# A two-layer attention trunk: TensorE in program order in the first attention, 24 conditioning columns on TensorE, a third raw buffer, bias vectors on 128 partitions

## The chip, the cores and the metric

The kernel runs on one core of one Trainium2 chip. The metric is the device time of one execution in microseconds (us). The core has five engines with a queue each: TensorE (PE in the profile, with PEld for its weight loads), VectorE (DVE), ScalarE (ACT), GpSimd (POOL) and SyncE (SP), which only issues DMAs here. ACT issues a few DMAs too. Each queue is worked off in order.

## The reference, cut to what matters

A decoder trunk of two layers, 512 tokens by 1024 features, float32. Each layer's input, residual gate and MLP are set by a conditioning vector c. Layer 0 has two sparse attentions in parallel (NSA with 8 heads, DSA with 8 heads), layer 1 a differential attention; a squared-ReLU MLP follows each.

```python
def reference(x, c, rel_bias, ada_w, ada_b, ...):
    c_act = jax.nn.silu(c)
    for l in range(DEPTH):                                   # 2
        ada = c_act @ ada_w[l] + ada_b[l]                    # 1024 x 6144 a layer
        sh1, sc1, g1, sh2, sc2, g2 = jnp.split(ada, 6, axis=-1)
        h = modulate(x, sh1, sc1)
        if l % 2 == 0:
            y = even_mixer(h, ..., rel_bias)                 # NSA and DSA
        else:
            y = diff_mixer(h, ..., rel_bias, lambda_init)
        x = layer_norm(ALPHA * x + (1.0 + g1[:, None, :]) * y, ln_g[l, 0], ln_b[l, 0])
        h = modulate(x, sh2, sc2)
        y = sq_relu_mlp(h, mlp_w1[l], mlp_w2[l])
        x = layer_norm(ALPHA * x + (1.0 + g2[:, None, :]) * y, ln_g[l, 1], ln_b[l, 1])
    return x
```

A bias from a table of 32 buckets by 16 heads, picked by the distance of two tokens, is added to every attention logit.

## The kernel before

**Weights.** All weights go through one stream (`Stream`, from line 107), a list of items of 128 partitions by 1024 floats (512 KB). `issue` (L134) puts the next items' DMAs on SP's queue as long as a raw buffer is free. There are two lasting raw buffers (`raw0`, `raw1` in `run`), four early ones that leave the pool when the items 24 and after "dq3" are reached, and later ones in tiles of other uses. `prepare` makes of a raw item two float32r parts: the first a cast on ACT (L265), the second a subtraction (L266) on DVE or, in the first attention, mostly on POOL. A product is three matmuls, first by first, first by second, second by first (`mm3`, L350 to L352). Items of kind "w" (compression weights, `cw1`) are used from the raw buffer itself, at most four at a time.

**Conditioning.** `ada` has 48 columns of 128 values a layer; each column of layer 0 is an item. Columns 0 to 15 (shift and scale of the first input) are needed first and are multiplied and summed on DVE (L250). Columns 16 to 39 of layer 0 (the gate, then shift and scale of the MLP) have two ways: a product on POOL (L247) with a sum on ACT (L248), which 21 take, or L250 on DVE for the three in `PLAN['ax']`. Their bias is added per eight columns (`ada_bias`, L407). Columns 40 to 47 of layer 0 and all of layer 1 go through `ada_pair` on TensorE: for two columns, eight matmuls with 32 output columns (L422), an ACT copy out of PSUM (L425), two one-column matmuls on that copy (L427), and a DVE addition of the bias (L428). A pair holds two raw buffers until it is done. `gate_row` spreads a gate over the partitions with 8 matmuls (L438).

**Stages.** From 0 to some 60 us, `even` loops over eight weight blocks "b1": modulated input (L1051 to L1053), then the projections in eight PSUM banks. After the eighth block `bias_write` follows its modulation on ACT's queue: a DMA of the bias vectors (L606) and two of the decay vectors (L608). They had been made by `bias_vectors` (L603: one-hot matmuls of the table, in 16 and 8 partitions) and are written to DRAM with 23 and 8 repeats; `gtile` (L537) and `cmp_bias` (L1214) read them back on SP's queue as bias tiles.

Then come slots of a software pipeline written out by hand, some 50 for NSA and, in a second loop, 19 for DSA. In a slot of NSA stand: gating (L1277, POOL), scores (`s0`: L504, L505), softmax pieces on DVE (L514) and ACT (L517), probabilities transposed (`s2`: L1479) two slots later, products with the values (`pv`: L1297, L1305) four slots later, and pieces of the index scores (L1157) and of a top-k of 16 rounds (L1183, L1184), both on DVE. The projections left ("iq", "ks", ... in the order of `PLAN['ord']`, then "dq0" to "dq3") and the block compression (L1527, in eight steps) are fills: a list with due slots (`Fill`), from which each slot takes its share. `latent_t` (L1106) is a fill behind "vc". An "a" in `ord` is the place of one of the columns 16 to 23 among the items; columns 24 to 39 stand behind the output weights ("eo0" to "eo3", four each).

**Order.** What the code says is the program order. A planner then sets the order of every engine's queue from its own costs: an instruction whose inputs it takes as ready may go ahead of one that the code has earlier. `add_manual_dep` with NoSync, or `issue_after`, lets an instruction stand behind another in the queue without a wait.

## Time and profile before

| | us |
|---|---|
| median of 3 runs | 1448.98 (1446.71 to 1451.75) |
| the profiled execution | 1449.99 |
| its span | 1448.2 |
| PE busy | 1342.0 (93%) |
| PEld busy | 1124.3 (78%) |
| DVE busy | 1143.5 (79%) |
| ACT busy | 658.8 (45%) |
| POOL busy | 581.0 (40%) |

The span is what the trace covers, from its first instruction to its last. Busy times of one engine are unions, so they never exceed the span. In the chain of work that ended last PE has 67% of the span, DVE 19%, DMA 4%. The first attention with its projections lies between 60 and 380 us; layer 0's MLP follows until some 770, layer 1's attention until some 1060, its MLP until the end. A line number in a row is that of the kernel before. "SPq" or "ACTq" is a queue's own instruction, mostly the issue of a DMA.

### The profile page before, as it was taken

Reading aid. Unit: us, or ns where it says so; the run is one execution under the profiler, and the core shown is the slowest. Engines: PE = TensorE matmul, PEld = TensorE weight load, DVE = VectorE, ACT = ScalarE, POOL = GpSimd, SP = SyncE. Lnnn points to the kernel's source line nnn. Section 1 sums busy time; section 2 is a strip of 40 time slices with the busy share of each in tenths; the row PEclk is TensorE's granted clock in tenths of the full one; section 3 lists DMA queues with packets and bytes.
Section 4 is the critical chain, followed back from the end, with each engine's and each line's share of the span. In section 5 each row is a group of like instructions: output and inputs, shape, how many; then the busy total and the mean of one; then the engine's idle time right before and its main releaser. Section 6 shows DMA issues by size and latency. Waiting matters only on the chain.

```text
span 1448.2 us, 22535 instructions
## 1 busy us (share of the span) xinstructions
PE 1342.0 (93%) x8286; PEld 1124.3 (78%) x8286; DVE 1143.5 (79%) x2185; ACT 658.8 (45%) x1412; POOL 581.0 (40%) x432
## 2 busy tenths in 40 slices
PE   6979998899899999999999799999979899999985
PEld 4758666676589888888887687887769789999974
DVE  6678979767578778878789825888975997898898
ACT  2455565746355333333332536776565443333321
POOL 2242677716432444444453622124164523122234
PEclk9989999999999999999999899999989999999997
DMA  9852432423731554444542442332350233323311
GB/s 333 247 165 94 152 104 90 131 72 106 258 132 37 183 178 172 175 175 161 189 163 91 149 153 92 102 103 78 137 166 14 90 100 117 110 70 113 116 59 58
DMA packets 58625, 189.47 MB, mean 131 GB/s; under 512 B 7778, under 2 KB 8482, under 8 KB 58516
## 3 DMA queue, kind: packets, MB, share of 16 engines
q1 hardware_dynamic: 55840, 184.67, 37.5%
q10 hardware_dynamic: 2676, 3.38, 1.1%
q8 instruction: 65, 1.06, 0.3%
q14 instruction: 44, 0.36, 0.1%
HBM read 178.42 MB, written 9.60 MB: 130 GB/s over the span
## 4 chain that ended last, share of the span: by engine, by line
PE 67%; DVE 19%; DMA 4%; issue 4%; ACT 3%; POOL 2%; SPq 0%; DVEq 0%; ACTq 0%; POOLq 0%
PE ps_mm L350 9%; PE ps_mm L351 9%; PE ps_mm L352 9%; PE ps_o L350 4%; PE ps_o L351 4%; PE ps_o L352 4%; PE ps_s L350 3%; PE ps_s L351 3%; PE ps_s L352 3%; PE ps_t L352 2%; PE ps_t L350 2%; PE ps_t L351 2%; DVE b L266 2%; PE ps_s L504 2%; PE ps_o L1297 2%
## 5 line engine op out<-in xcount | busy, mean ns | idle before, releaser
L350 PE MATMUL ps_mm<-hT,b 128*128 128x256 f32 (+1 forms) x560 | 190.9, 343 | 19.2 <-ACT b L265 13.1
L351 PE MATMUL ps_mm<-hT,b 128*128 128x256 f32 (+1 forms) x560 | 189.5, 339 | 5.4 <-DVE hT L717 5.1
L352 PE MATMUL ps_mm<-hT,b 128*128 128x256 f32 (+1 forms) x560 | 188.7, 338 | 1.8 <-DVE b L220 1.8
L350 PEld LDWEIGHTS ps_mm<-hT,b 128*128 128x128 f32 x560 | 108.5, 194 | 35.3 <-ACT b L265 13.1
L351 PEld LDWEIGHTS ps_mm<-hT,b 128*128 128x128 f32 x560 | 108.7, 194 | 18.1 <-DVE hT L717 5.6
L220 POOL TENSOR_TENSOR b<-s,b 128x512 fp32r<-128x512 f32 x33 | 46.9, 1423 | 183.6 <-ACT b L219 179.7
L517 ACT ACTIVATE z<-z,st 128x128 f32<-128x128 f32 (+3 forms) x160 | 89.3, 559 | 65.2 <-DVE st L514 56.5
L896 POOL TENSOR_TENSOR ot<-z,ot 128x512 fp32r<-128x512 f32 x39 | 61.3, 1572 | 141.4 <-ACT ot L895 127.8
L352 PEld LDWEIGHTS ps_mm<-hT,b 128*128 128x128 f32 x560 | 108.3, 194 | 12.0 <-DVE b L220 2.0
L350 PE MATMUL ps_o<-b,ot 128*128 128x512 f32 x251 | 101.1, 403 | 4.0 <-ACT b L265 2.3
L351 PE MATMUL ps_o<-b,ot 128*128 128x512 f32 x251 | 99.9, 398 | 2.9 <-DVE b L266 2.9
L731 DVE TENSOR_TENSOR u<-ps_o,u 128x512 f32<-128x512 f32 x121 | 82.3, 680 | 22.9 <-PE ps_o L352 22.6
L352 PE MATMUL ps_o<-b,ot 128*128 128x512 f32 x251 | 99.3, 396 | 0.0
L514 DVE CUSTOM_DVE_ANT_0 z<-ps_s,g 128x128 f32<-128x128 f32 (+3 forms) x160 | 75.2, 484 | 24.6 <-PE ps_s L505 19.0
L265 ACT CAST b<-raw 128x1024 fp32r<-128x1024 f32 (+1 forms) x62 | 64.3, 1042 | 61.6 <-issue 14.4
L266 DVE TENSOR_TENSOR b<-s,b 128x1024 fp32r<-128x1024 f32 x47 | 70.6, 1505 | 18.7 <-ACT b L265 18.3
L265 ACT CAST b<-s 128x1024 fp32r<-128x1024 f32 x47 | 49.0, 1048 | 78.1 <-PE ps_t L351 15.8
L266 DVE TENSOR_TENSOR b<-raw,b 128x1024 fp32r<-128x1024 f32 (+1 forms) x42 | 55.3, 1318 | 33.6 <-ACT b L265 33.3
L350 PE MATMUL ps_s<-b,ot 128*128 128x512 f32 x181 | 72.8, 402 | 0.0
L351 PE MATMUL ps_s<-b,ot 128*128 128x512 f32 x181 | 72.0, 398 | 0.0
L731 DVE TENSOR_TENSOR u<-ps_s,u 128x512 f32<-128x512 f32 x87 | 59.2, 681 | 15.8 <-PE ps_s L352 15.6
L352 PE MATMUL ps_s<-b,ot 128*128 128x512 f32 x181 | 71.6, 396 | 0.0
(471 smaller groups left out, 4241.4 us busy)
## 6 DMA issues: line engine op xcount, KB each, us to landing
s<-mlp_w SPq DMA_DIRECT2D x55, 512.0 KB
s<-ada_p SPq DMA_DIRECT2D x39, 512.0 KB
s<-mlp_wp SPq DMA_DIRECT2D x33, 512.0 KB
raw<-ada_w SPq DMA_DIRECT2D x23, 512.0 KB
raw<-mlp_w SPq DMA_DIRECT2D x21, 512.0 KB
raw<-mlp_wp SPq DMA_DIRECT2D x19, 512.0 KB
early<-ada_w SPq DMA_DIRECT2D x17, 512.0 KB
raw<-ada_p SPq DMA_DIRECT2D x17, 512.0 KB
```

Source lines behind the costliest of these rows:

```text
L220: (nc.gpsimd if PLAN["sl"][it.l][n] else nc.vector).tensor_tensor(out=lo, in0=src, in1=f32(hi), op=ALU.subtract)
L265: nc.scalar.copy(out=hi.cols(c.start, w), in_=raw[:, c])
L266: getattr(nc, ("vector", "gpsimd")[PLAN["lo"][it.name]] if it.name in PLAN["lo"] else k.lo_engine).tensor_sub(out=lo.cols(c.start, w), in0 ...
L350: mm(ps, lhsT=l[0], rhs=r[0], start=start, stop=False)
L351: mm(ps, lhsT=l[0], rhs=r[1], start=False, stop=False)
L352: mm(ps, lhsT=l[1], rhs=r[0], start=False, stop=stop)
L504: mm(ps, lhsT=q[:, qs], rhs=k[0][:, ks], start=start, stop=False)
L514: i = nc.vector.tensor_tensor_reduce(out=z[:, :w], in0=ps, in1=bias, scale=-1.0, scalar=3e38, op0=ALU.add, op1=ALU.min, accum_out=st[:, m: ...
L517: j = nc.scalar.activation(out=z[:, :w], in_=z[:, :w], func=AF.Exp, scale=-1.0, bias=st[:, m:m + 1], accum_out=st[:, 2 + m:3 + m])
L731: self.nc.vector.tensor_add(out=u[:, sl], in0=ps, in1=u[:, sl])
L896: (nc.gpsimd if PLAN["hl"][l][f % 2] else nc.vector).tensor_tensor(out=hl[:, c0:c1], in0=r[:, c0:c1], in1=f32(hh[:, c0:c1]), op=ALU.subtract)
L1297: nc.tensor.matmul(o[ab], lhsT=V[:, br, j, 64 * ab:64 * ab + 64], rhs=pts[ab][br][:, 128 * j:128 * j + 128], start=i % 2 == 0 and br == 0 ...
```

## The change

It has four parts. (1) TensorE's instructions are traced through `InOrder`, which, where `on` is set, puts each behind the one before it: from the first slot of NSA to the end of DSA TensorE issues in program order. Before and after that the planner's order stays. (2) Columns 16 to 39 of layer 0 go through `ada_pair`, so the old branch on POOL and ACT, `PLAN['ax']` and `ada_bias` go; the eight "a" stand in twos in `ord`, and the host's layout of the columns follows. `cact`, now needed for columns 0 to 15 alone, shares the space of the gate rows. (3) A third lasting raw buffer. (4) The table is repeated eight times over its columns, so that the one-hot matmuls give the bias vectors on 128 partitions and the decay vectors on 64; the vectors are written with 3 repeats from each of 128 partitions (24 in all, for 23), the decay vectors once from each of 64; and the writes stand behind the seventh modulation instead of the eighth.

The diff, cut to its core (further lines that only replace `nc.tensor` by `self.pe_` are left out):

```diff
 PLAN = {...
- 'ax': ((0, 19), (0, 36), (0, 38)),
...
- 'ord': ('iq', 'a', 'ks', 'n0', 'a', 'kw', 'a', 'a', 'a', 'a', 'kc', 'vc', 0, 'a', 1, 2, 3, 'n1', 4, 5, 'a', 6, 7,
+ 'ord': ('iq', 'a', 'a', 'ks', 'n0', 'kw', 'a', 'a', 'a', 'a', 'kc', 'vc', 0, 'a', 'a', 1, 2, 3, 'n1', 4, 5, 6, 7,
          'n2', 'n3'),
...
-NREP = 23
+NREP = 24
...
             if not k.ada_pe(l, m):
-                acc = k.adac[:, l, m:m + 1]
-                if bool(16 <= m < 48) != ((l, m) in PLAN["ax"]):
-                    nc.gpsimd.tensor_tensor(out=raw, in0=raw, in1=k.cact, op=ALU.mult)
-                    nc.scalar.activation(out=raw, in_=raw, func=AF.Copy, scale=0.5, accum_out=acc)
-                else:
-                    nc.vector.scalar_tensor_tensor(out=raw, in0=raw, scalar=0.5, in1=k.cact, op0=ALU.mult,
-                                                   op1=ALU.mult, accum_out=acc)
+                nc.vector.scalar_tensor_tensor(out=raw, in0=raw, scalar=0.5, in1=k.cact, op0=ALU.mult,
+                                               op1=ALU.mult, accum_out=k.adac[:, l, m:m + 1])
...
+class InOrder:
+    def __init__(self, tc):
+        self.tc, self.pe, self.on, self.last = tc, tc.nc.tensor, False, None
+
+    def put(self, i):
+        if self.on and self.last is not None:
+            self.tc.add_manual_dep(i.ins, self.last.name,
+                                   mybir.DependencyInfo(mybir.DependencyClass.NoSync, mybir.DependencyReason.DATA), reason="in order")
+        self.last = i.ins
+        return i
+
+    def matmul(self, *a, **kw):
+        return self.put(self.pe.matmul(*a, **kw))
+
+    def transpose(self, *a, **kw):
+        return self.put(self.pe.transpose(*a, **kw))
...
+        self.pe_ = InOrder(tc)
...
-        mm = self.nc.tensor.matmul
+        mm = self.pe_.matmul
...
-    def ada_bias(self, l, sp):
-        sl = slice(8 * sp, 8 * sp + 8)
-        self.nc.vector.tensor_add(out=self.adac[:, l, sl], in0=self.adac[:, l, sl], in1=self.adab[:, l, sl])
...
-        return l > 0 or m >= 40
+        return l > 0 or m >= 16
...
-        return self.a["ada_p"][8 + m if l else m - 40] if self.ada_pe(l, m) else self.a["ada_w"][m]
+        return self.a["ada_p"][32 + m if l else m - 16] if self.ada_pe(l, m) else self.a["ada_w"][m]
...
-        self.cact = C.tile([128, 1024], F32, name="cact")
+        self.cact = self.B.tile([128, 1024], F32, tag="grow", bufs=1, name="cact")
...
-        sb = [self.s4()[:16, :HB] for _ in range(2)]
+        sb = [self.s4()[:, :HB] for _ in range(2)]
 
         def go():
+            rep = self.z()[:33, :192]
+            nc.vector.tensor_copy(out=rep.rearrange("p (m r) -> p m r", r=8), in_=tab[:, :, None].to_broadcast([33, 24, 8]))
             for i, c0, n, m, t0 in ((0, 0, 512, 16, 0), (0, 512, 128, 16, 0), (0, NVEC, HB - NVEC, 8, 16),
                                     (1, 0, 512, 8, 16), (1, 512, HB - 512, 8, 16)):
                 p = self.bank("t")
-                nc.tensor.matmul(p[:m, :n], lhsT=tab[:, t0:t0 + m], rhs=oh[i][:, c0:c0 + n], start=True, stop=True)
-                nc.vector.tensor_copy(out=sb[i][:m, c0:c0 + n], in_=p[:m, :n])
+                self.pe_.matmul(p[:8 * m, :n], lhsT=rep[:, 8 * t0:8 * t0 + 8 * m], rhs=oh[i][:, c0:c0 + n],
+                                 start=True, stop=True)
+                nc.vector.tensor_copy(out=sb[i][:8 * m, c0:c0 + n], in_=p[:8 * m, :n])
         def write():
-            nc.scalar.dma_start(out=self.bvec, in_=sb[0][:, None, :NVEC].to_broadcast([16, NREP, NVEC]))
-            for x, c in ((sb[0][:8, NVEC:], slice(0, HB - NVEC)), (sb[1][:8], slice(HB - NVEC, 16 * NDEC))):
-                nc.scalar.dma_start(out=self.bdec[:, :, c], in_=x[:, None, :].to_broadcast([8, 8, x.shape[1]]))
+            c = NREP // 8
+            nc.scalar.dma_start(out=self.bvec.rearrange("h (r c) n -> (h r) c n", c=c),
+                                in_=sb[0][:, None, :NVEC].to_broadcast([128, c, NVEC]))
+            for x, c in ((sb[0][:64, NVEC:], slice(0, HB - NVEC)), (sb[1][:64], slice(HB - NVEC, 16 * NDEC))):
+                nc.scalar.dma_start(out=self.bdec.rearrange("h r n -> (h r) n")[:, c], in_=x)
...
-            if k == 7:
+            if k == 6:
                 with self.tc.issue_after(act.ins):
                     bias_write()
...
         self.phase = "n"
+        self.pe_.on = True
...
-                self.ada_bias(0, 2)
...
+        self.pe_.on = False
         self.phase = None
         self.lo_engine = "vector"
         for m in (3, 4):
             st.get(I["adaE", 8 * m + 7])
-            self.ada_bias(0, m)
...
-            for s in range(2):
+            for s in range(3):
                 st.raws.append((self.W.tile([128, 1024], F32, name=f"raw{s}"), 1 << 30))
```

## Rows read from the trace of the kernel before

**Rows 1.** Windows: stretch, length; PE, PEld, DVE, ACT, POOL busy; clock; DMA.

```profile
20.00:40.00 20.00, 19.68 (x90) 15.54 (x90) 18.13 (x32) 5.49 (x7) 0.98 (x1) 1.00 0.95 350
60.00:130.00 70.00, 57.62 (x319) 45.62 (x320) 49.58 (x93) 36.60 (x83) 22.78 (x12) 0.85 0.51 152
130.00:190.00 60.00, 55.69 (x420) 43.07 (x420) 57.35 (x168) 30.55 (x75) 32.50 (x31) 0.94 0.41 135
190.00:300.00 110.00, 99.59 (x693) 73.97 (x692) 90.11 (x285) 69.99 (x187) 78.87 (x73) 0.94 0.33 109
300.00:380.00 80.00, 71.15 (x435) 53.01 (x434) 52.49 (x138) 43.84 (x110) 35.99 (x33) 0.97 0.38 120
```

**Rows 2.** The chain that ended last, 0 to 130 us: start, length, what.

```profile
49.48 11.88 DMA bvec<-s
...
66.86 9.87 DMA raw<-ada_w
...
91.85 0.43 PE ps_mm L350
...
99.47 0.23 PE ps_mm L350
```

**Rows 3.** Timeline of ACT, 44 to 100 us: start, length, what [idle, releaser].

```profile
49.48 0.82 ACT L1051 ACTIVATE hT<-z,mod 128x512 fp32r<-128x512 f32 x1 [2.08 <-DVE mod L1049]
...
50.20 5.58 ACTq L608 DMA_DIRECT2D bdec<-s  x2
55.90 1.05 ACT L265 CAST b<-early 128x1024 fp32r<-128x1024 f32 x1 [5.60 <-issue]
...
67.94 1.05 ACT L265 CAST b<-early 128x1024 fp32r<-128x1024 f32 x1 [7.09 <-DMA early<-ev_b]
```

**Rows 4.** The timeline of PE, 44 to 100 us.

```profile
62.30 0.79 PE L350 MATMUL ps_mm<-hT,b 128*128 128x512 f32 x1 [2.77 <-DVE q L373]
...
86.63 0.91 PE L1106 MATMUL ps_t<-ident,ot 128*128 128x128 f32 x3 [6.32 <-DVE ot L1099]
```

**Rows 5.** Lines 247, 248, 250 (ns min/median/max); line 247's window.

```profile
L247 POOL TENSOR_TENSOR raw<-raw,cact x16: 2344/2376/2420, 73.8 to 293.1; 128x1024 f32<-128x1024 f32 x16
...
L248 ACT ACTIVATE raw<-raw x16: 1041/1048/1064, 76.9 to 296.5; 128x1024 f32<-128x1024 f32 x16
...
L250 DVE SCALAR_TENSOR_TENSOR raw<-raw,cact x7: 1205/1220/1807, 15.6 to 286.5; 128x1024 f32<-128x1024 f32 x7
...
190.00:300.00 110.00, 32.83 (x14) 0.94 0.33 109
```

**Rows 6.** The timelines of POOL and DVE, 214 to 228 us, and line 1236 over the span.

```profile
215.23 2.37 POOL L247 TENSOR_TENSOR raw<-raw,cact 128x1024 f32<-128x1024 f32 x1
...
215.18 0.55 DVE L529 COPY s<-ps_t 128x384 f32<-128x384 f32 x1
...
215.91 1.72 DVE L1236 TENSOR_SCALAR cst<-cst 128x4 f32<-128x4 f32 x1
...
L1236 DVE TENSOR_SCALAR cst<-cst x8: 154/226/1715, 152.2 to 245.7; 128x4 f32<-128x4 f32 x8
```

**Rows 7.** Pairs on TensorE: the chain, 376 to 394 us, and line 425 over the span.

```profile
385.82 0.54 PE ps_mm L427 x4
...
389.81 1.86 PE ps_mm L422 x32
...
L425 ACT COPY z<-ps_mm x4: 365/372/372, 384.7 to 391.7; 128x256 f32<-128x256 f32 x4
```

**Rows 8.** The timeline of SP, 125 to 420 us.

```profile
310.85 23.00 SPq L537 DMA_DIRECT2D g<-bvec  x3
```

**Rows 9.** The chain that ended last, 300 to 430 us.

```profile
333.94 5.45 DMA raw<-ev_out
...
366.86 4.43 DMA s<-mlp_w
```

**Rows 10.** The timeline of PE, 150 to 185 us.

```profile
165.52 0.79 PE L504 MATMUL ps_s<-k,q 128*128 128x512 f32 x1 [2.51 <-DVE st L514]
```

More of the change, by code (lines that the diff above doesn't have):

```diff
@@ L437, in row @@
                 c = 4 * h + k
-                nc.tensor.matmul(ps[:, 128 * k:128 * k + 128], lhsT=col[:, c:c + 1].to_broadcast([128, 128]), rhs=self.ident,
+                self.pe_.matmul(ps[:, 128 * k:128 * k + 128], lhsT=col[:, c:c + 1].to_broadcast([128, 128]), rhs=self.ident,
                                  start=True, stop=True)
@@ L502, in scores @@
     def scores(self, ps, q, k, qs, ks, start=True):
-        mm = self.nc.tensor.matmul
+        mm = self.pe_.matmul
         mm(ps, lhsT=q[:, qs], rhs=k[0][:, ks], start=start, stop=False)
@@ L1227, in cmp_a @@
                 for o in range(0, 128, m):
-                    nc.tensor.matmul(ps[o:o + m, 32 * s:32 * s + 32], lhsT=f32(nq[4 * k + s])[:, 128 * i + o:128 * i + o + m],
+                    self.pe_.matmul(ps[o:o + m, 32 * s:32 * s + 32], lhsT=f32(nq[4 * k + s])[:, 128 * i + o:128 * i + o + m],
                                      rhs=kc[:, 32 * (s % 2):32 * (s % 2) + 32], start=True, stop=True)
@@ L1296, in pv @@
                     for ab in range(2):
-                        nc.tensor.matmul(o[ab], lhsT=V[:, br, j, 64 * ab:64 * ab + 64], rhs=pts[ab][br][:, 128 * j:128 * j + 128],
+                        self.pe_.matmul(o[ab], lhsT=V[:, br, j, 64 * ab:64 * ab + 64], rhs=pts[ab][br][:, 128 * j:128 * j + 128],
                                          start=i % 2 == 0 and br == 0 and j == 0, stop=False)
@@ L1304, in pv @@
                 for ab in range(2):
-                    nc.tensor.matmul(po[p][64 * ab:64 * ab + 64], lhsT=box["cmp", 1][rs, 64 * ab:64 * ab + 64],
+                    self.pe_.matmul(po[p][64 * ab:64 * ab + 64], lhsT=box["cmp", 1][rs, 64 * ab:64 * ab + 64],
                                      rhs=pc[p // 2][rs, hs], start=False, stop=True)
@@ L1399, in s0 @@
                 if i:
-                    nc.tensor.matmul(ps[:, :w], lhsT=self.negr, rhs=drop[i][:, :w], start=True, stop=False)
+                    self.pe_.matmul(ps[:, :w], lhsT=self.negr, rhs=drop[i][:, :w], start=True, stop=False)
                 self.scores(ps[:, :w], dq[p][ab], dk[p][ab], slice(128 * i, 128 * i + 128), slice(0, w), not i)
@@ L1427, in pv @@
                     for ab in range(2):
-                        nc.tensor.matmul(po[64 * ab:64 * ab + 64], lhsT=Vd[:, j, p, 64 * ab:64 * ab + 64], rhs=PT[p][ab][:, c:c + 128],
+                        self.pe_.matmul(po[64 * ab:64 * ab + 64], lhsT=Vd[:, j, p, 64 * ab:64 * ab + 64], rhs=PT[p][ab][:, c:c + 128],
                                          start=j == 0, stop=j == i)
@@ L1493, in pv @@
                 o = po[64 * ab:64 * ab + 64]
-                self.nc.tensor.matmul(o if both else o[:, 128:], lhsT=v[j], rhs=y, start=j == 0, stop=j == n - 1)
+                self.pe_.matmul(o if both else o[:, 128:], lhsT=v[j], rhs=y, start=j == 0, stop=j == n - 1)
     def compress_in(self, ps, kv):
@@ L1526, in compress @@
                             m = 64 if 1 else 128
-                            nc.tensor.matmul(pss[k][o:o + m], lhsT=w[:, cs + o:cs + o + m], rhs=xl[:, :, 4 * c + li],
+                            self.pe_.matmul(pss[k][o:o + m], lhsT=w[:, cs + o:cs + o + m], rhs=xl[:, :, 4 * c + li],
                                              start=c == 0 and li == 0, stop=c == 3 and li == 3)
@@ L1552, in compress @@
                 if kv == 0:
-                    nc.tensor.matmul(ps[:, :64], lhsT=w2[:, 128 * k:128 * k + 128],
+                    self.pe_.matmul(ps[:, :64], lhsT=w2[:, 128 * k:128 * k + 128],
                                      rhs=h[:, k, 0].rearrange("p g n -> p (g n)"), start=k == 0, stop=k == 1)
                 else:
-                    nc.tensor.matmul(ps[:, :64], lhsT=h[:, k].rearrange("p d g n -> p (d g n)"),
+                    self.pe_.matmul(ps[:, :64], lhsT=h[:, k].rearrange("p d g n -> p (d g n)"),
                                      rhs=w2[:, 256 + 64 * k:320 + 64 * k], start=k == 0, stop=k == 1)
@@ L1685, in s3 @@
                 v = V[h // 4][j // 2][:, 512 * (j % 2) + c:512 * (j % 2) + c + 128]
-                nc.tensor.matmul(po[h][:, i], lhsT=pt[:, js], rhs=v, start=j == 0, stop=j == i)
+                self.pe_.matmul(po[h][:, i], lhsT=pt[:, js], rhs=v, start=j == 0, stop=j == i)
             if i == 3 or h == 7:
```

18 lines of the change are left out of this document (9 added, 9 removed).

## The prediction

> **What bounds the kernel now.** I read the windows view first, for the stretch that the change touches: from 60 us, when the first projection ends, to 380 us, when the first attention's output is normalised. [rows 1] cuts it in four. TensorE is busy 57.62 of 70, 55.69 of 60, 99.59 of 110 and 71.15 of 80 us, so it stands idle 12.4, 4.3, 10.4 and 8.9 us, 36 us in all. DVE is nearly full once, 57.35 of 60 us in 130 to 190. No engine bounds the whole stretch: the first part waits, the second is DVE's, the rest is mostly TensorE's.
>
> Then I read the chain of waits at the opening [rows 2]. From 49.48 the chain is a DMA, the write of the bias vectors, 11.88 us for 920 KB, that is 77 GB/s. SP's queue goes through a read of those vectors to a conditioning load that takes 9.87 us. ACT shows the same congestion [rows 3]: its two issues of the decay vectors last 5.58 us, the cast behind them waits 5.60 us, and a later cast waits 7.09 us for its weights. TensorE pays with 2.77 us of idling at 62.30 and 6.32 us at 86.63 [rows 4]; the granted clock averages 0.85 in 60 to 130 [rows 1], and the spacing of a 512-column matmul is 0.43 us at 91.85 against 0.23 us at 99.47 [rows 2].
>
> Third, the conditioning columns themselves [rows 5]: a column on the old path is 2.38 us of POOL and 1.05 us of ACT, or 1.22 us of DVE. The plan puts 21 of the 24 on POOL and ACT, 3 on DVE. In [rows 6] a POOL product runs from 215.23 for 2.37 us and a four-element DVE operation beside it takes 1.72 us; the same line has a median of 0.226 us. POOL's product thus holds up DVE.
>
> **The change part by part.** The profiled execution took 1449.99 us (span 1448.2); the median of the runs shown is 1448.98, 1.0 us lower. The sum is made on the first and 1.0 us is taken off at the end.
>
> *Bias vectors on 128 partitions, written one step earlier.* The write goes from 920 to 960 KB, the decay writes stay at 264 KB. The rate is bounded below by the 77 GB/s of [rows 2] and above by the 350 GB/s that the loads reach in 20 to 40 us [rows 1]: 1.22 MB take 3.5 to 16 us. I take some 5 us, near the upper rate, because the sources then lie on all partitions, as those of the loads do. One more small DVE copy (33 partitions by 192) costs at most the 0.55 us of a 384-column copy [rows 6]; it comes before the first projection, where the tables' DMAs end last. On ACT's queue the three issues move from behind the eighth modulation to behind the seventh; the cast of the last weight block and the eighth modulation are queued behind them. The eighth waited 2.08 us for DVE anyway [rows 3]: issues up to that long cost nothing, the old 5.58 us would cost 3.5. What can be won is TensorE's idling in 60 to 130, 12.4 us [rows 1], and the lowered clock: a mean of 0.85 between 1.2 and 2.4 GHz is 21 of the 70 us at 1.2 GHz, and where TensorE runs in them, say in half, each matmul takes 0.43 us for 0.23, so 5 us can come back. From 0 to 17 us. Four of the twelve new pairs fall here too and use about 9 us of that room (next but one), so I take -9 us with these four paid.
>
> *POOL, ACT and DVE set free.* 21 products of 2.38 us leave POOL (50 us), 21 x 1.05 us leave ACT (22 us, of which twelve copies of 0.37 us return), 3 x 1.22 us leave DVE, with three small bias additions; twelve additions of two columns come. Most of it was cover already. What counts is DVE held up in 190 to 300, where 14 products run for 32.8 us [rows 5]: if each held DVE for the 1.5 us of [rows 6] and DVE were the path throughout, 21 us; if DVE is never the path, nothing. DVE is busy 90.11 of 110 there, TensorE 99.59 [rows 1], so about a quarter counts: -5 us.
>
> *Twelve pairs on TensorE.* [rows 7] shows the same routine for later columns: 32 records, two pairs, take 1.86 us, so 0.93 us a pair, and its two one-column matmuls 0.54 us: 1.47 us a pair, 17.6 us for twelve. In program order the one-column matmuls stand directly behind the eight, and wait for an ACT copy of 0.37 us. Nothing else can go between. The wait is 0.4 us at least and 1.8 us where a cast of some 1.05 us is ahead on ACT; transposes, scores and projections are queued behind it. So 1.9 to 3.3 us a pair; I take 2.3. The other eight pairs, 18.6 us, fall into 190 to 300, where TensorE idles 10.4 us. The bounds are 8 x 1.9 - 10.4 = +5 and 8 x 3.3 = +26; I take +13, because idle time that is spread over waits covers only part.
>
> A page weighs against this. TensorE's busy share in 190 to 300 leaves 10.4 us of room, its weight loads 36 us (73.97 of 110, [rows 1]). The Trainium skill, "Perfetto Trace Analysis", section "Identifying the Most-Contended Engine", says that matmul occupancy is a poor measure because matmuls are pipelined, and that weight-load occupancy should be used. By that the eight pairs would fit and cost nothing; it is the third rival below.
>
> *A third raw buffer.* SP's queue stands 23.00 us before the reads of the bias rows at 310.85 [rows 8], and the load of the output weights behind it then takes 5.45 us on the chain; a first MLP weight takes 4.43 us at 366.86 [rows 9]. With one more buffer these loads are issued before that wait, or one item sooner. From 0 to -9.9 us; I take -5. A pair holds two buffers until it is done, which is why the third is not worth more. Later stages hold few DMA waits and get 0.
>
> *Program order.* In the stretch before, the planner lets TensorE run ahead: at 86.63 it stands before the transposes of the latent, which the code queues behind the "vc" projection, while index scores of earlier slots are still to come; at 165.52 it stands 2.51 us before scores [rows 4, 10]. Those scores are behind DVE, which program order does not cure; other work that was ready is what it can put there. Outside the opening the idling is 23.6 us [rows 1]. Order could win about half, 12 us. It could also lose: each projection's first matmul waits for its weight's second part, which POOL makes in some 2.4 us, as long as a product [rows 5], and the stretch has thirteen projections (scores and transposes are queued behind them): at half of it 16 us. I take -6.
>
> Sum: -9 - 5 + 13 - 5 - 6 = -12, so 1438.0 us profiled and 1437 us in the median.
>
> **The rivals.** *Slower: TensorE stands at the head of its own queue.* If ACT's casts are in the way of each pair's copy, the pairs cost their upper bound, +26, and order loses 5 instead of winning 6, while the other gains stay: -9 - 5 - 5 + 26 + 5 = +12, 1461 us. For it: 93% busy share in 130 to 190 and 91% in 190 to 300, and the turn-round has no cover. Against: ACT is busy only 69.99 of 110 us and gets lighter. It decides from the point at which pairs and order together cost more than the 19 us of the rest.
>
> *No change: DVE takes what is won.* DVE has 57.35 of 60 us in 130 to 190 and its index and top-k work is unchanged. What is won before 130 then turns into TensorE waiting for DVE: -3 instead of -9, -3 instead of -5, +13, -5, -2: 0, 1449 us. Against: TensorE feeds DVE, and before 130 DVE idles too, 49.58 of 70.
>
> *Faster than forecast: the pairs fit.* Eight pairs in the 36 us of room that the weight loads leave: the +13 becomes 0, the sum -25, 1424 us. Against it, in the chain TensorE's pieces follow each other closely in 190 to 300; for it, half of those pieces run at a lowered clock (0.94 in the mean).
>
> *The change doesn't do what it says*, if the order is kept but the planner fills the other queues so that it gives the same times: it is the forecast without its -6, and lies within the forecast's case.
>
> **How the numbers follow.** About 0.3%, 4.3 us, is what a measurement of this kernel can tell from no change. Forecast (1437): 0.43. Pairs fit (1424): 0.21. No change (1449): 0.15. Slower (1461): 0.21. The range reaches down to -9 more on the opening (its bound of 17, rounded up) and -5 on loads from the third rival, 1410, and up to the slower rival, 1461: below 1 in 10 is left on either side. Faster 0.64, same 0.15, slower 0.21.
>
> **What the profile after would show.** Right: the bias write under 6 us; no ACT issue over 3 us near 46; TensorE idle in the 70 us after the first projection under 6 us; no POOL product and no DVE stretch beside it; pairs of 1.5 us with under 1 us of idling before their one-column matmuls; no load of output weights on the chain. Wrong: TensorE idle before the one-column matmuls for over 1.8 us; long idling before projections that waits for POOL's second part; a first attention in which DVE is 95% busy from 100 to 200 with TensorE waiting; or a bias write that still takes over 10 us.

## The result: 2.9% slower

The changed kernel takes 1488.52 us in the median of four executions (1486.87 to 1495.55) against 1447.85 us before (four executions): a ratio of 1.029, 95% interval 1.0256 to 1.0324. The forecast was 1437 us and the range ended at 1461, so the sign was wrong and the time lies outside the range. The execution profiled after took 1489.86 us, its span is 1488.1 us, 39.9 us longer than before.

All of the loss arises in the first attention. The first statistics of the norm that follows it start at 369.7 us before and at 409.9 us after, 40.2 us later; at the end of the span the distance is 39.9 us. So the same windows as in [rows 1] are the place to look.

The windows of the kernel after (stretch, length; PE, PEld, DVE, ACT, POOL busy; clock; DMA):

```profile
60.00:130.00 70.00, 58.56 (x385) 45.50 (x385) 47.26 (x99) 33.88 (x74) 9.89 (x6) 0.93 0.45 143
130.00:190.00 60.00, 40.58 (x322) 32.65 (x319) 50.64 (x149) 23.44 (x60) 23.61 (x24) 0.83 0.34 103
190.00:300.00 110.00, 92.75 (x742) 71.98 (x741) 72.34 (x258) 50.49 (x146) 38.44 (x56) 0.88 0.21 70
300.00:380.00 80.00, 70.94 (x465) 54.28 (x464) 41.66 (x112) 35.87 (x90) 18.62 (x20) 0.98 0.27 93
```

From 130 to 300 us every engine is *less* busy than in [rows 1] (part of that is the change's own doing on POOL and ACT, which lost the columns). From 130 to 190 us TensorE fell from 55.69 to 40.58 us of 60, DVE from 57.35 to 50.64; from 190 to 300 TensorE fell from 99.59 to 92.75 although four pairs of columns came to it. In this stretch no engine has become the bound; the engines wait for each other. The granted clock fell with it, from 0.94 to 0.83 and from 0.94 to 0.88.

What TensorE waited for after, 55 to 420 us (engine, line, releaser: us in total, times, longest):

```profile
PE ps_mm L297 <- ACT z L436: 8.0, 12, 1.8
PE ps_o L297 <- issue: 8.0, 1, 8.0
PE ps_s L297 <- DVE ot L484: 6.8, 1, 6.8
PE ps_s L297 <- ACT z L1219: 6.8, 7, 4.3
PE ps_mm L297 <- DMA raw<-ada_p: 6.7, 2, 4.7
PE ps_mm L297 <- DVE raw L256: 4.8, 1, 4.8
PE ps_t L300 <- POOL z L1265: 4.7, 2, 3.2
PE ps_o L297 <- DVE ot L1567: 3.3, 1, 3.3
```

There is no single cause: a few long waits for DVE, ACT, POOL and DMA, in all 65.0 us (365 less the 299.98 busy) against 40.2 us before. In time they stand as follows (the timeline of PE after: start, length, what, idle before it and its releaser):

```profile
68.62 1.19 PE L297 MATMUL ps_s<-q,ot 128*128 128x512 f32 x2 [6.77 <-DVE ot L484]
139.16 1.09 PE L297 MATMUL ps_o<-ot 128*128 128x64 f32 x4 [7.97 <-issue]
151.84 0.39 PE L297 MATMUL ps_s<-k,q 128*128 128x256 f32 x1 [4.30 <-ACT z L1219]
180.93 1.09 PE L297 MATMUL ps_o<-ot 128*128 128x64 f32 x4 [3.28 <-DVE ot L1567]
234.51 1.31 PE L300 MATMUL ps_t<-ident,z 128*128 128x128 f32 x3 [3.19 <-POOL z L1265]
248.59 1.94 PE L297 MATMUL ps_mm<-raw,ccol 128*32 128x256 f32 x16 [4.67 <-DMA raw<-ada_p]
283.82 1.51 PE L297 MATMUL ps_mm<-raw,ccol 128*32 128x256 f32 x12 [4.75 <-DVE raw L256]
```

The longest is worth reading through. At 139.16 the last matmuls of the first compression start after 7.97 us of idling. They multiply what the compression's hidden layer gives after its activation, a run of small DVE and ACT pieces. The same stretch on DVE (timeline of DVE after):

```profile
131.90 0.68 DVE L1201 MAX8 m<-ot 128x8 f32<-128x512 f32 x1
...
132.69 0.68 DVE L1202 MATCH_REPLACE8 ot<-m,ot 128x512 f32<-128x512 f32 x1
133.77 2.11 DVE L1557 TENSOR_TENSOR z<-z 128x124 f32<-128x124 f32 x1 [0.41 <-ACT z L1556]
135.81 0.68 DVE L1201 MAX8 m<-ot 128x8 f32<-128x512 f32 x1
136.41 0.20 DVE L1558 TENSOR_SCALAR z<-z 128x124 f32<-128x124 f32 x1
...
138.85 0.21 DVE L1567 TENSOR_SCALAR ot<-z 128x124 f32<-128x124 f32 x1
```

The activation's pieces (lines 1557 to 1567) alternate with the top-k search (lines 1201, 1202), and one of them takes 2.11 us. The last piece ends at 139.06, and 0.1 us later TensorE goes on, although the profile names no releaser ("issue"). TensorE stands 8 us for 1.1 us of matmuls, and index scores, projections and the next units stand behind them in the queue. The piece of 2.11 us runs beside a subtraction for a weight's second part on POOL (timeline of POOL after):

```profile
133.40 2.34 POOL L260 TENSOR_TENSOR b<-raw,b 128x1024 fp32r<-128x1024 f32 x1 [0.42 <-ACT b L259]
```

### The profile page after: what moved, and what is told of

Same layout as the page of the kernel before. It is cut to its first block, busy times and chain, and to the rows that moved or that the text cites. A ratio compares the mean times of both kernels' runs of the same rounds, so it can differ in the third digit from the quotient of the medians.

```text
span 1488.1 us, 22990 instructions
## 1 busy us (share of the span) xinstructions
PE 1350.9 (91%) x8526; PEld 1133.9 (76%) x8526; DVE 1137.1 (76%) x2189; ACT 642.8 (43%) x1382; POOL 523.4 (35%) x411
## 4 chain that ended last, share of the span: by engine, by line
PE 73%; DVE 15%; DMA 4%; ACT 4%; issue 3%; POOL 2%; ACTq 0%; DVEq 0%; SPq 0%; POOLq 0%
PE ps_mm L297 31%; PE ps_o L297 16%; PE ps_s L297 15%; PE ps_t L297 7%; PE ps_t L300 3%; DVE b L260 2%; DVE u L749 1%; ACT b L259 1%; DMA raw<-ev_out 1%; DVE b L219 1%; DVE m L1201 1%; POOL b L260 1%; DVE ot L1202 1%; DVE z L525 1%; DVE hT L735 1%
## 5 line engine op out<-in xcount | busy, mean ns | idle before, releaser
L297 PE MATMUL ps_mm<-hT,b 128*128 128x256 f32 (+1 forms) x1680 | 333.9, 344 | 23.8 <-ACT b L259 13.4
L297 PEld LDWEIGHTS ps_mm<-hT,b 128*128 128x128 f32 x1680 | 265.5, 196 | 61.2 <-ACT b L259 13.4
L297 PE MATMUL ps_o<-b,ot 128*128 128x512 f32 x753 | 199.5, 395 | 4.5 <-DVE b L260 3.0
L297 PEld LDWEIGHTS ps_o<-b,ot 128*128 128x128 f32 x753 | 133.8, 188 | 33.7 <-DVE b L260 3.8
L297 PE MATMUL ps_s<-b,ot 128*128 128x512 f32 x543 | 145.8, 397 | 0.0
L297 PEld LDWEIGHTS ps_s<-b,ot 128*128 128x128 f32 x543 | 98.3, 191 | 18.4 <-DVE u L749 0.5
L297 PE MATMUL ps_mm<-b,ot 128*128 128x512 f32 x384 | 100.9, 410 | 7.1 <-DVE u L749 6.1
L297 PEld LDWEIGHTS ps_mm<-b,ot 128*128 128x128 f32 x384 | 72.3, 196 | 24.5 <-DVE u L749 7.3
L297 PEld LDWEIGHTS ps_t<-q,b 128*128 128x128 f32 x504 | 66.5, 188 | 4.4 <-DVE b L219 0.4
L297 PE MATMUL ps_t<-q,b 128*128 128x256 f32 x504 | 69.2, 282 | 0.1
```

The costliest lines, as they stand in the source:

```text
L297: return self.put(self.pe.matmul(*a, **kw))
```

## The experiments

Two questions: which part of the change loses, and by what mechanism. All ratios are to the kernel before on the same chip.

### Which part: each part undone or done alone

**Without the order.** The changed kernel, everything but the order kept:

```diff
-        self.pe_.on = True
```

> The changed kernel with the planner's order on TensorE again; columns, third buffer and bias vectors as changed. Theory A (program order lets TensorE stand at the head of its own queue, and costs more than all of the loss): 1430 us, 18 below the kernel before, since the opening's gain of some 10 us and POOL's freed time stay. Theory B (the columns on TensorE cost: loads and turn-round of the pairs): 1475 to 1485 us. Theory C (only both together cost: the pairs' waits have no cover in program order): 1440 to 1450 us.

Measured: 1452.14 us against 1452.1, ratio 1.0007 (0.9983 to 1.003). None of the theories names this time: A is 22 us too low, B 23 too high, C 2 too low. The order costs the whole loss, 36 us by the medians and 41 by the ratios (the two kernels come from two series, each beside the kernel before); the other three parts together are worth nothing that can be measured. The same stretches without the order (windows):

```profile
130.00:190.00 60.00, 56.35 (x454) 44.15 (x452) 54.98 (x174) 31.75 (x82) 31.95 (x32) 1.00 0.37 118
190.00:300.00 110.00, 104.86 (x806) 73.99 (x802) 74.84 (x251) 52.86 (x151) 41.82 (x55) 0.94 0.32 105
```

In 130 to 190 TensorE is busy 56.35 us and gets 454 matmul records done where the changed kernel gets 322. At the compression the same chain of small pieces takes as long: its hidden matmuls end at 128.66, its last ones start at 137.14, 8.5 us later (8.0 with the order). But here TensorE idles only 0.61 us of it, because projections, scores and the spreading of a gate stand in front (timeline of PE without the order):

```profile
134.23 0.91 PE L297 MATMUL ps_mm<-hT,b 128*128 128x512 f32 x3
134.99 1.05 PE L297 MATMUL ps_mm<-ident,adac 128*128 128x128 f32 x8
...
137.14 0.63 PE L297 MATMUL ps_o<-ot 128*128 128x64 f32 x4 [0.61 <-PE ps_t L300]
```

Up to the first statistics of the norm the two kernels have nearly the same number of matmul records. The windows from 55 us to that point, with the order and without:

```profile
55.00:409.90 354.90, 293.48 (x2096) 227.46 (x2095) 237.00 (x674) 165.01 (x421) 111.05 (x120) 0.91 0.33 104
```

```profile
55.00:376.10 321.10, 303.69 (x2085) 225.44 (x2085) 230.89 (x673) 162.73 (x421) 114.24 (x120) 0.95 0.36 118
```

With the order TensorE idles 61.4 us and is busy 293.5; without it 17.4 and 303.7. So the 33.8 us between them are 44 us of more idling less 10 us of busy time: by the profile the loss is idling, not slower matmuls.

**The order alone.** The kernel before with the class InOrder and its calls, switched on and off where the change does it:

```diff
-                nc.tensor.matmul(ps[:, 128 * k:128 * k + 128], ...
+                self.pe_.matmul(ps[:, 128 * k:128 * k + 128], ...
...
+        self.pe_.on = True
...
+        self.pe_.on = False
```

> The kernel before with TensorE in program order from the first slot of NSA to the end of DSA, and nothing else. Theory A: 1490 us or more, that is, 40 to 55 us above the kernel before. Theory B: 1440 to 1455 us. Theory C: 1450 to 1465 us, since no pair is in the ordered stretch.

Measured: 1481.21 us, ratio 1.0209 (1.0164 to 1.0254), +29 us. That is 9 us less than theory A's least and 16 or more above B and C: the order loses with the old columns too. TensorE stands 76.3 us between 55 and 420 us, and in one wait for what the change takes away: at 139.7 for ACT's part of a column (line 248), 7.18 us.

**The order in the first half of the stage only.** Switched off before the second of the stage's two attentions (the one that the top-k search masks):

```diff
         ck = box["ck"]
+        self.pe_.on = False
```

> The changed kernel with the order ended between NSA and DSA. The trace of the changed kernel has the first softmax piece of DSA 34.7 us after the last one of NSA, against 7.1 us before. Theory A with its larger part at that join: 1460 us (28 us back). Theory A with its loss inside NSA (20 us are lost there by the last NSA softmax): 1480 us. Theory B: no change, 1488 us.

Measured: 1483.86 us, ratio 1.023 (1.0191 to 1.0269). Some 5 to 9 us of the loss come from the second attention (the intervals of the two ratios overlap, so this share is not clear of noise); the rest, 32 us against no order, from the first, where compression, projections, index scores, top-k and three branches interleave.

**The bias vectors alone.** The kernel before, with the write from 128 partitions one step earlier and nothing else:

```diff
+            rep = self.z()[:33, :192]
...
-            nc.scalar.dma_start(out=self.bvec, in_=sb[0][:, None, :NVEC].to_broadcast([16, NREP, NVEC]))
+            nc.scalar.dma_start(out=self.bvec.rearrange("h (r c) n -> (h r) c n", c=c),
+                                in_=sb[0][:, None, :NVEC].to_broadcast([128, c, NVEC]))
...
-            if k == 7:
+            if k == 6:
```

> The kernel before with the bias vectors on 128 partitions and their write one step earlier, and nothing else. Theory F (the opening's gain of 10 us at the latent's end stays, and the columns eat it in the kernel without order): 1440 us, 8 to 12 below. Theory G (the gain is gone by the first softmax piece of NSA, as in the kernel without order, where it is 0.1 us at that point): 1447 to 1454 us, the same as before.

Measured: 1442.32 us against 1448.82, ratio 0.9936 (0.9913 to 0.9958). This part wins 6.5 us, less than theory F's 8 to 12 and more than G's nothing, and this kernel is faster than both. The windows of 56 to 62 us, first of the kernel before, then of this one:

```profile
56.00:62.00 6.00, 3.52 (x18) 2.85 (x16) 3.04 (x3) 4.85 (x7) 2.40 (x1) 0.97 0.94 123
```

```profile
56.00:62.00 6.00, 6.00 (x30) 5.33 (x29) 2.39 (x3) 3.42 (x5) 2.41 (x1) 1.00 0.94 282
```

The DMA engines are as busy in both (0.94), but they move 282 GB/s instead of 123, and TensorE no longer stands. The two windows don't hold the same transfers. Before, the write is on its way until 61.36 us [rows 2]; here it is issued at 48.21, and SP, which waits for it (`DMA bvec<-s`), issues the first read of it at 55.80:

```profile
55.80 1.35 SPq L537 DMA_DIRECT2D g<-bvec  x2
```

So the write takes some 7.6 us for 960 KB instead of 11.88 for 920, and ends 5.6 us earlier. The spread over the partitions and the earlier place were changed together; no run separates them. The last transpose of the latent starts 5.2 us earlier (84.26 us, before 89.42), and 6.9 us of lead are left at the end of the span.

**The columns, with and without the third buffer.** The changed kernel without the order and with the old bias vectors; then the same with two buffers:

```diff
-            for s in range(3):
+            for s in range(2):
```

> The kernel before with the columns on TensorE and the third raw buffer; old bias vectors, planner's order. Theory F: 1460 us, 8 to 12 above before, since the columns cost what the bias vectors bring. Theory G: 1450 to 1456 us, about the same as before.

> As cols_raw3, with two raw buffers as before. If the third buffer is worth the 5 us of the prediction: 5 us above cols_raw3. If pairs with two buffers have to wait for each other's loads: 10 to 25 us above it. If the buffer is worth nothing: the same as cols_raw3.

Measured: with three buffers 1454.85 us, ratio 1.0045 (1.0024 to 1.0067), +6 us; with two 1468.24 us, ratio 1.0117 (1.0091 to 1.0143), +19 us. The third buffer is worth 13.4 us by the medians, 10.4 by the ratios, once the columns are on TensorE. With the 6.5 us of the bias vectors, the +6.0 of the columns with three buffers makes the nothing that all three parts gave together. The groups of the pairs' matmuls, 55 to 310 us (busy, mean ns, idle before and releaser), with two buffers:

```profile
L297 PE MATMUL ps_mm<-raw,ccol 128*32 128x256 f32 x144 | 12.2, 411 | 8.5 <-DMA raw<-ada_p 8.5
L297 PE MATMUL ps_mm<-sel,z 128*128 128x1 f32 x42 | 7.2, 273 | 1.1 <-ACT z L436 1.1
L297 PE MATMUL ps_mm<-early,ccol 128*32 128x256 f32 x32 | 2.3, 387 | 4.9 <-issue 4.7 <-DVE adac L439 0.2
```

and with three:

```profile
L297 PE MATMUL ps_mm<-raw,ccol 128*32 128x256 f32 x160 | 11.1, 385 | 0.2 <-DVE adac L439 0.2
L297 PE MATMUL ps_mm<-sel,z 128*128 128x1 f32 x44 | 7.4, 269 | 1.1 <-ACT z L436 1.1
L297 PE MATMUL ps_mm<-early,ccol 128*32 128x256 f32 x16 | 1.3, 385 | 0.0
```

With two buffers TensorE waits 13.2 us before pairs: 8.5 for loads, and 4.7 for which the profile names no releaser. With three it does not wait for a load at all. The work itself is 21.7 and 19.8 us. The third buffer without the columns was not tried.

### By what mechanism: who is late, or that nothing may pass

Four theories of the order's cost: the pairs' turn-round carries it (the slower rival of the prediction); the late pieces named above carry it; DVE makes them late, with top-k rounds that run ahead or with top-k as a whole; or, whoever is late, the order takes away what TensorE could do meanwhile, and the next late instruction takes the place of each one that is mended.

**Pairs outside the order; compression and compressed branch outside the order.** In two kernels, one call each as it was:

```diff
 def ada_pair(...)
-        nc, mm = self.nc, self.pe_.matmul
+        nc, mm = self.nc, self.nc.tensor.matmul
```

> The changed kernel with the matmuls of the pairs left out of the order, so that the planner places them; all else keeps program order. Theory A: 1480 us or more, as twelve turn-rounds of 0.65 to 1.8 us make 8 us of TensorE's idling. Theory B and C: 1450 to 1465 us, as the pairs' waits for loads (17 us in three of them) and copies get cover.

```diff
 compression, last matmuls (kv 0 and 1); cmp_c
-                    self.pe_.matmul(ps[:, :64], ...
+                    nc.tensor.matmul(ps[:, :64], ...
-            self.pe_.transpose(pt[:, :128], cb, self.ident)
+            nc.tensor.transpose(pt[:, :128], cb, self.ident)
```

> The changed kernel with three kinds of TensorE instructions left out of the order: the last matmuls of each block compression and the transposes of the compressed branch's probabilities. In the changed kernel TensorE idles 8.0 and 3.3 us before the first two compressions end and 4.7 us before such transposes, 16 us of 65 in 55 to 420 us. Theory D (a few late instructions at the queue's head cost what TensorE idles there, and no more): 1470 to 1475 us. Theory E (whichever instruction is late next takes the place, as with the pairs left out, which gained nothing): 1483 to 1500 us.

Measured: the first 1498.1 us, ratio 1.0332 (1.0292 to 1.0373), no faster than the changed kernel; the second 1484.59 us, ratio 1.023 (1.0199 to 1.0261). So the pairs are not the carrier: their wait for ACT's copy is 8.0 us in twelve in the list above, 0.7 us each. (For loads and prepared buffers the list has 14.2 us in four waits before pairs, 6.7, 4.8 and 2.7, not 17 in three.) And of the 16.0 us of waits before the instructions freed in the second (8.0, 3.3 and 4.7 in the list above) 4 us came back by the medians, 9 by the ratios. The timeline of PE in the second, where the changed kernel waits 4.67 us for a load:

```profile
241.03 1.94 PE L297 MATMUL ps_mm<-raw,ccol 128*32 128x256 f32 x16 [4.54 <-DVE ot L1202]
```

The compression's waits are gone, but three of 2.0 to 2.5 us stand in their place, the wait before this pair has only another releaser, and the branch's transposes still come after 3.19 us although they are free; TensorE idles 54.8 us, 10 less. So a quarter to a half of what these waits cost did come back: theory E's range holds the time, but theory D is not wholly wrong.

**Top-k behind the softmax.** Each round is kept behind the last softmax maximum placed before it:

```diff
-            ta = 0
+            ta = 1
```

> The changed kernel, with one edit: each round of the top-k search on DVE is kept behind the softmax maximum that the program placed last before it, so that the 48 rounds can no longer run ahead. In the changed kernel the last round ends near 165 us of the trace (194 us before), between the pieces of the compression that TensorE, in order, stands waiting for. Theory F (rounds running ahead delay the late pieces on DVE, and the order makes TensorE stand for each): TensorE's idle time between 55 and 420 us falls from 65 us by 10 or more and the time from about 1488 us to 1470 to 1480. Theory E (the order itself, whoever is late: the next late instruction takes the place of each one mended): within 5 us of the changed kernel, 1483 to 1493.

Measured: 1496.62 us, ratio 1.0331 (1.0299 to 1.0364), nothing won, and 4 us above theory E's range. The rounds do run later: the last match-replace starts at 301.6 us, against 248.2 in the changed kernel and 258.5 before (the expectation's 165 is where two of the three blocks of rows are done). But the edit does not touch the longest wait, 7.69 us here: the rounds of the first block stand between the compression's pieces as they did. So this run speaks against rounds that run ahead in general, not against those at the compression; the next pair of runs does.

**Two of sixteen rounds, in order and free.**

```diff
-            todo = [i for i in only if rounds.get(i, 16) < 16]
+            todo = [i for i in only if rounds.get(i, 2) < 2]
...
-            if r == 15:
+            if r == 1:
...
```

> The changed kernel with 2 of the 16 top-k rounds for each of three blocks of rows (42 of 48 rounds, some 1.4 us of DVE each in two instructions of 0.3 to 0.7 us, are left out, so the sparse attention selects fewer keys to drop and the output differs). Read beside the same reduction without the order: the difference of the two is what the order costs when DVE has some 50 us less to do in the stage. Theory F (DVE's top-k rounds make the late pieces late): the order then costs under 15 us of the 37 that it costs with all rounds. Theory E (any work of another engine on the way is late for an engine that stands in order two slots behind): it still costs 25 us or more.

> The changed kernel without the order on TensorE, with 2 of the 16 top-k rounds for each of three blocks of rows (42 of 48 rounds are left out, so the output differs): the partner of the reduced kernel in order. DVE is some 95 per cent busy from 130 to 190 us in the kernel before; were DVE the bound of the stage without the order, about 30 to 45 us would go (1407 to 1422 us); if TensorE is, under 10 (1442 to 1452).

Measured: in order 1484.82 us (ratio 1.024, 1.0206 to 1.0273), free 1442.66 us (0.996, 0.9937 to 0.9982), beside a kernel before of 1449.35. The order costs 42 us with 42 of 48 rounds taken away, no less than with all of them. DVE's load does not carry it. At the compression, where no round stands between the pieces any more, TensorE still waits 6.28 us (timeline of PE, in order):

```profile
139.53 1.08 PE L297 MATMUL ps_o<-ot 128*128 128x64 f32 x4 [6.28 <-ACT z L1560]
```

The windows of 55 to 420 us, in order and free:

```profile
55.00:420.00 365.00, 309.93 (x2228) 239.81 (x2226) 198.46 (x569) 169.69 (x431) 119.82 (x128) 0.92 0.36 118
```

```profile
55.00:420.00 365.00, 350.55 (x2475) 264.89 (x2475) 228.05 (x621) 193.00 (x492) 139.22 (x140) 0.98 0.41 135
```

Free, TensorE idles 14.5 us; in order 55.1 us, with DVE busy little more than half of the time.

**A deeper pipeline.** Transposes three slots behind the scores, products five:

```diff
-        e2, e3 = (2, 4)
+        e2, e3 = (3, 5)
```

> The changed kernel with the first attention's hand-written pipeline one slot deeper: the transposes of a unit's probabilities stand three slots behind its scores instead of two, the products with V five instead of four. Theory D (the depth written by hand is too shallow for an engine that may not look ahead): the transposes' and products' waits shrink, and the time falls by 10 us or more, to under 1478. Theory E: the waits at the compression, at the compressed branch, at the pairs and at the scores stand in other steps of the slot and stay; the time is within 6 us of the changed kernel's, or worse, since the deeper pipeline holds its buffers longer.

Measured: 1496.03 us, ratio 1.0328 (1.0301 to 1.0355), no faster than the changed kernel. The long waits stand where they stood, in other steps of the slot (7.76 us at 136.7 before the compression's last matmul).

**The order by degrees.** Each instruction is kept behind the one K places before it in the program (K = 8, 32, 128, 512; the changed kernel is K = 1):

```diff
-            self.tc.add_manual_dep(i.ins, self.last.name,
+            self.tc.add_manual_dep(i.ins, self.last[-K].name,
...
-        self.last = i.ins
+        self.last.append(i.ins)
```

> The changed kernel with a looser order: each TensorE instruction stands behind the one 8 places before it in the program, not behind the last one. Between 55 and 420 us the changed kernel has 2136 matmuls in 365 us, so 8 places are some 1.4 us of work. The order costs 36 us in all (1488 against 1452). Theory E-near (what is lost is ready work just behind a late instruction; TensorE's longest waits are 2 to 8 us): a quarter to a half of it comes back, 1470 to 1480. Theory E-far (what is lost is work brought forward from far behind): nothing comes back, 1484 to 1492.

> As before with 32 places, some 5.5 us of work at the same rate. Theory E-near: most of the 36 us is back, 1455 to 1466. Theory E-far: at most a quarter, 1478 to 1490.

> As before with 128 places, some 22 us of work, longer than any single wait of TensorE in the changed kernel (8.0 us). Theory E-near: all of it is back, 1448 to 1456, the time without the order. Theory E-far: about half, 1465 to 1475.

> As before with 512 places, some 88 us of work, a quarter of the stage. Both theories: the time without the order, 1448 to 1456. If it is still slower by 10 us or more, the scheduler had brought work forward over more than that, or the manual dependency has a price of its own, whatever it orders.

Measured:

| places that an instruction may be taken early | us | ratio to before (95%) | TensorE idle, 55 to 420 us |
|---|---|---|---|
| 1 (the change) | 1488.52 | 1.029 (1.0256 to 1.0324) | 65.0 |
| 8 | 1502.12 | 1.036 (1.0324 to 1.0396) | 46.1 |
| 32 | 1469.17 | 1.013 (1.0094 to 1.0166) | 31.1 |
| 128 | 1458.61 | 1.0059 (1.0026 to 1.0092) | 24.2 |
| 512 | 1453.67 | 1.0039 (1.0017 to 1.0062) | 23.6 |
| any | 1452.14 | 1.0007 (0.9983 to 1.003) | 22.0 |

The windows of 55 to 420 us behind the last column, for 8 and for 32 places:

```profile
55.00:420.00 365.00, 318.88 (x2104) 232.79 (x2102) 235.44 (x681) 167.52 (x424) 111.97 (x120) 0.89 0.32 102
```

```profile
55.00:420.00 365.00, 333.95 (x2262) 243.71 (x2261) 243.59 (x708) 172.30 (x442) 126.65 (x132) 0.94 0.37 124
```

From 32 places on, the freedom that is given back brings the time back with it: a little over half of the order's loss with 32 places (1.6 of 2.8%), four fifths with 128, nine tenths with 512. With 512 places there are as many added dependencies as with one, so they have no price of their own above the 0.3% that is left. The "near" theory has the larger part, but its forecast for 32 places (1455 to 1466) was missed by 3 us and that for 128 by 3 us: some of what is lost may be work brought forward over more than 128 places. Eight places are slower than one by 14 us (0.7% by the ratios), which no theory expected. TensorE idles 19 us less there in the window, but its work takes longer: up to the first statistics of the norm (416.5 us) it is busy 316.30 us for 2082 records, where the changed kernel is 293.48 for 2096. The granted clock is 0.89 against 0.91. As an estimate from these two means, some 4% more of 360 us is then spent at 1.2 instead of 2.4 GHz, 14 us in which half the work is done: some 7 of the 23 us. Where the rest comes from stays open.

One thing holds for all these runs. The planner sets the queues of the other engines too, and sets them anew for each kernel; no run holds them fixed. How much of the loss is TensorE's own queue, and how much is other engines and loads that the planner then placed later, is not separated.

## Why the prediction was wrong

**The step that failed is the program order: -6 us was taken, with a bound of +16, and it costs +36 or more.** It went wrong twice.

First, the idle time was read the wrong way. The prediction took the 23.6 us of idling outside the opening as what an order could win. But that idling was what was left after the planner had put ready work, most of it from up to some hundred places further on (the order by degrees), in front of instructions that come late. Without the order and with the rest of the change the idling from 55 to 420 us is 22.0 us, with it 65.0 us: 43 us more, and 36 to 41 us of time. For the same work it is 44 us. The wait of [rows 10], 2.51 us before scores, was read correctly as one that order does not cure; but nowhere did the prediction ask the reverse: what work stands in front of a late instruction that order forbids.

Second, the bound was set by one named wait, that of each projection for its weight's second part from POOL, priced at half of thirteen times 2.4 us. (By the order of the three products it would be the second matmul, not the first, that needs the second part.) That wait does not occur. The largest group of the projections in the kernel after, 55 to 420 us:

```profile
L297 PE MATMUL ps_mm<-hT,b 128*128 128x512 f32 x320 | 95.3, 434 | 1.0 <-DVE adac L439 0.6 <-ACT k L500 0.4
```

Of their idling of 1.0 us none is for POOL, and in the whole of TensorE's waits of 55 to 420 us none is for a second part. What TensorE stood for was what the prediction never priced: the compression's last matmuls (11.3 us), the index scores behind a DVE split (6.8), scores behind ACT (6.8), the loads of the pairs (9.4) and the compressed branch's transposes (4.7). To bound an order from the trace, every producer with a latency that other engines set had to be counted, not one kind. Of the four signs named for being wrong none came but for one wait of 1.81 us before one-column matmuls, a hair over the 1.8 named (DVE is 83% busy from 100 to 200); they did not cover this case either.

**The slower rival had the mechanism and not the carrier.** "TensorE stands at the head of its own queue" is what happened. Its price hung on the pairs' copy, 26 us, and 5 us of order; the copy's waits are 8.0 us in all, inside the 0.4 to 1.8 us each that was foreseen, and taking the pairs out of the order won nothing. "DVE takes what is won" did not come either: DVE is busy 50.64 of 60 us from 130 to 190, less than before, and without the order 42 of its 48 top-k rounds were worth 0.5% (0.996 against 1.0007).

**The other parts, against the measured ones.** Together -6 was forecast without the order (-9, -5, +13, -5); 0 was measured (-2.5 to +4.4 by its interval). That the sum is nearly right is partly luck: the third buffer and the columns missed in opposite directions.

- Opening, -9 with four pairs paid: the bias vectors alone bring -6.5. The working was not consistent: a bound of 17 less some 9 for the pairs leaves 8, not 9, and the range then counted the 17 as if no pair had to be paid. One sign came: the three issues on ACT take 2.57 us together, and the cast behind them waits 1.91 us instead of the 5.60 of [rows 3] (timeline of ACT after):

```profile
46.09 0.62 ACTq L623 DMA_DIRECT2D bvec<-s  x1
46.74 1.95 ACTq L626 DMA_DIRECT2D bdec<-s  x2
48.81 1.92 ACT L259 CAST b<-early 128x1024 fp32r<-128x1024 f32 x2 [1.91 <-issue]
```

  "Under 6 us" for the write did not come: it takes some 7.6 us with the bias vectors alone, and in the kernel after at most 8.8 (issued at 46.09, first read at 54.85). TensorE's idling in 60 to 130 was to fall under 6 us and is 11.4 us, as the order put 6.77 us of waiting there; without the order it is 7.0 us, so this sign fails even then.
- Columns, +13, and engines set free, -5: +8 forecast, +19.4 measured with two buffers and +6.0 with three. A pair costs 1.7 to 1.8 us without waits (20.9 us in 55 to 310 us without the order, 12.2 + 7.4 + 1.3: eight-matmul groups of twelve pairs, one-column matmuls of eleven), a little over the 1.47 us of [rows 7]. Of the eight pairs placed in 190 to 300, seven fell there without the order and four with it (and their 18.6 us should read 18.4, 8 x 2.3). What the freed engines gave back was not measured by itself. The POOL products beside DVE are gone, but a small DVE operation still takes up to 2.40 us (line 1254, at 165.73 us; median 0.17). Beside it, as beside the 2.11 us at 133.77, POOL runs a subtraction of 128 x 1024 (line 260, 165.74, 2.37 us). So what the reading of [rows 6] says of products goes, in these two cases, for POOL's subtractions as well, and those the change left there.
- Third buffer, -5: worth 10 to 13 us, because of the columns and not, as forecast, because of the later loads. The sentence "a pair holds two buffers until it is done, which is why the third is not worth more" had it upside down: with both buffers held, no load can run ahead. The load of the output weights is still on the chain after (DMA on the chain of waits, 300 to 460 us), beside the 5.45 us of [rows 9]:

```profile
327.95 4.42 DMA raw<-ev_out
```

  and SP's reads of the bias rows are still drawn out over 19.00 us, beside the 23.00 us of [rows 8] (timeline of SP after). In [rows 8], too, that time lies among the three reads and not before them; one waits 21.6 us for a softmax piece on DVE.

```profile
353.48 19.00 SPq L548 DMA_DIRECT2D g<-bvec  x4
```

  Without the order the reads are drawn out over 21.61 us, yet the chain from 300 to 400 us holds no DMA among its 95 longest pieces: without the order that sign came.

- "The pairs fit": the weight loads left 36 us of room [rows 1] for eight pairs. The Trainium skill, "Perfetto Trace Analysis", section "Identifying the Most-Contended Engine", would judge TensorE's headroom by its weight loads (and by MFU, which no run here gives) and not by its matmul busy time. In the run without the order TensorE's busy time in 190 to 300 rises from 99.59 to 104.86 us, with seven pairs in it, while its weight loads stay at 73.99, and the columns with three buffers cost 6.0 us, about a third of their work. So by this case the room was partly there; it was not free.

## What to carry to other kernels

An engine's idle time under a planner that reorders is not a reserve that a fixed order can win: ask of each wait what ready work now runs before it, and price an order by the late producers of *all* kinds in the stage. Where an order is wanted all the same, loosen it by degrees and measure: here 32 places of freedom still cost 1.2% against no order at all, 128 half a per cent, and 8 were no better than one. And when work moves to a route that holds two buffers per step, the buffers have to be counted as part of the price: the third was worth 10 to 13 us, where the columns with it cost 6.

## What was not expected of the hardware

Busy DMA engines say little about the rate: in 56 to 62 us the DMA share is 0.94 in both kernels, but 123 GB/s are moved while the write from 16 partitions is on its way, and 282 in the kernel in which it comes from 128 and is already over. And the clock was lowest where TensorE stood most: in 130 to 190 us the granted clock (of a full 2.4 GHz) was 0.83 with the order, 0.94 before and 1.00 without the order, at 40.58, 55.69 and 56.35 us of busy time. One matmul of the projections lasts 434 ns in the mean with the order and 408 without it (55 to 420 us), but over all kinds TensorE is busy 10 us less for the same work; what the lower clock costs by itself is not separated.
